# Leaving x un-normalised on chip and applying 1/rms where the products are read, in a hybrid decoder layer

## The chip, the core and the metric

The kernel runs on one core of a Trainium2 chip. The core has five engines, each working through its own queue in order: TensorE (PE in the profile) multiplies matrices, VectorE (DVE) and ScalarE (ACT) work on tiles, GpSimd (POOL) does a few small things, and SyncE (SP) issues most DMAs. An engine goes on only when what its next instruction needs has been signalled. The metric is the device time of one launch in microseconds, median of the runs.

## What is computed

A decoder layer over 256 tokens of width 2048, all in float32. The part that matters here is its entry:

```
h = rms_norm(x, norm_g)                  # x * rsqrt(mean(x*x) + eps) * g, per token
proj = h @ w_in                          # 2048 x 11264
q, k, v, z_a, u_b, v_b, z_b, g_a, g_b = split(proj)
q = rms_norm(q per head, q_norm_g);  k = rms_norm(k per head, k_norm_g)
att = moba_attention(q, k, v)
y_a = (att * silu(z_a)) @ w_proj_a
sgu = spatial_gating(gelu(u_b), gelu(v_b), ...)
y_b = (sgu * silu(z_b)) @ w_proj_b
merged = sigmoid(g_a) * y_a + sigmoid(g_b) * y_b
out = x + merged @ w_out
```

With 256 tokens the attention is plain causal attention inside one block. The factor 1/rms in the first line is one number per token, a row factor, so it can be applied to `x` before the product or to the rows of `proj` after it.

## The kernel before

**Products.** A float32 product is made of three matmuls of halves: every operand is split into a high half (ScalarE's cast to float32r, `wh`, `xh`) and a low half (VectorE's subtraction, `wl`, `xl`), and `three` (L302) issues low by high, high by high, high by low. Weights come as 120 steps of 1 MB (`schedule`, L50). In 104 of them a step is a 2 by 2 set of blocks: for half of these the block products are made as they stand (`direct`, L311: 24 matmuls of 128x512), the other half use seven products instead of eight (`seven`, L325: 21 matmuls), for which VectorE first adds weight blocks (`t`, L143 to L146) and splits more pieces (`wlp`, L155; `tl`, L157).

**Order of steps.** The first eight steps (0 to 7) make q, all direct. Then come k, v, za, vb, ub and zb with eight steps each, g with four chunks that alternate with the projections y, and out. Steps 8 to 15 are k, 16 to 23 are v. While step i is multiplied, step i + 2 is split and step i + 3 is fetched (L664 to L670). Rings of buffers bound how far this runs ahead: four `raw`, three `wh` and `wl`, two `whp` and `wlp`. For ScalarE and VectorE the order up to step 7 is written out by hand (`manual_schedule`, L639); behind it, and for the other engines, a scheduler sets the order when the kernel is built.

**x.** `x` arrives transposed (`xt`, features by tokens). `split_x` (L205) multiplies it by norm_g and splits it into `xuh`, `xul`, which serve q alone. For everything behind q the kernel normalises: `load_nat` (L191) fetches `x` once more by tokens, `stats` (L245) squares and sums it on ScalarE and takes 1/rms (`rsqrt`, L240: VectorE's mean plus eps, then GpSimd's power of -0.5) into `rstd`; `stats_row` (L250) turns `rstd` into a row with two PE transposes (`ps_R`); `normalise` (L258) multiplies `xt` by it in place on VectorE; and `halves_x` (L262) splits the result again into `xh`, `xl`. `forms` and `forms_4` (L272 to L299) make sums of blocks of the normalised `xt` for the seven-product steps. q itself, made from un-normalised halves, gets `rstd` as ScalarE's scale when it is read out (L695).

**Head norms.** `sums` (L376) squares q, k and vb per head on ScalarE and takes rsqrt of the sums; `norm_qk` (L389) applies it.

The dictionary `later`, filled by `at` (L576), says after which step each of these is issued; on SP, the fetch by tokens stands where `load_nat` is called.

Of the kernel before, what the change touches and what calls it, by code (L numbers as in the profile page):

```python
# [13 lines left out]
F32R = mybir.dt.float32r  # L14
# [6 lines left out]
P = 128  # L21
# [46 lines left out]
def hybrid_layer_kernel(  # L68
# [97 lines left out]
    xv = const.tile([P, NVEC + S], F32, name="xv")  # L166
    vec = xv[:, 0:NVEC]
    xt = [slot(F32, f"xt{i}").rearrange("p (k t) -> p k t", t=S) for i in range(2)]
    xu_h, xu_l = [], []

    def load_x(p0, p1):
        nc.sync.dma_start(xt[p0 // 8][:, p0 % 8:(p1 - 1) % 8 + 1, :],
# [20 lines left out]
            nc.sync.dma_start(xn[m], x[m * P:(m + 1) * P, :])  # L193

    for i in range(2):
        xu_h.append(slot(F32R, f"xuh{i}").rearrange("p (k t) -> p k t", t=S))
        xu_l.append(slot(F32R, f"xul{i}").rearrange("p (k t) -> p k t", t=S))

    warm = unit.tile([P, B], BF16, tag="u", name="warm")
    nc.vector.memset(warm, 0.0)  # L200
# [4 lines left out]
    def split_x(kp, js=None):  # L205
        i, a = kp // 4, 2 * (kp % 4)
        for j in js or range(2):
            src = xv[:, NVEC:] if kp + j == 0 else xt[i][:, a + j, :]
            nc.scalar.activation(xt[i][:, a + j, :], src, AF.Copy, scale=vec[:, 2 * kp + j:2 * kp + j + 1])
        sl = slice(a + js[0], a + js[0] + 1) if js else slice(a, a + 2)  # L210
        src = xt[i][:, sl, :]
        nc.scalar.copy(xu_h[i][:, sl, :], src)
        nc.vector.tensor_tensor(xu_l[i][:, sl, :], src, f(xu_h[i][:, sl, :]), op=ALU.subtract)

    ident = const.tile([P, P], F32, name="ident")
    make_identity(nc, ident)
# [17 lines left out]
        nc.sync.dma_start(gain, bass.AP(tensor=sg.tensor, offset=sg.offset, ap=[[0, P], [1, P]]))  # L234

    rstd = const.tile([P, 2], F32, name="rstd")
    R = xv[:, NVEC:]
    ssum = const.tile([P, 2], F32, name="ssum")

    def rsqrt(dst, src, n, count):  # L240
# [4 lines left out]
    def stats():  # L245
        for m in range(2):
            nc.scalar.activation(xn[m], xn[m], AF.Square, accum_out=ssum[:, m:m + 1])
        rsqrt(rstd, ssum, 2, D)

    def stats_row():  # L250
        ps = bank(0, "ps_R")
        for m in range(2):
            nc.tensor.transpose(ps[:, m * P:(m + 1) * P], rstd[:, m:m + 1].to_broadcast([P, P]), ident)
        nc.scalar.copy(R, ps[:, 0:S])

    xh, xl = [None, None], [None, None]

    def normalise(i):  # L258
        src = xt[i]
        nc.vector.tensor_tensor(src, src, R[:, None, :].to_broadcast([P, 8, S]), op=ALU.mult)  # L260

    def halves_x(i):  # L262
        xh[i] = slot(F32R, f"xh{i}").rearrange("p (k t) -> p k t", t=S)
        xl[i] = slot(F32R, f"xl{i}").rearrange("p (k t) -> p k t", t=S)
        nc.scalar.copy(xh[i], xt[i])
        nc.vector.tensor_tensor(xl[i], xt[i], f(xh[i]), op=ALU.subtract)

    def spare(t):

# [104 lines left out]
    def sums(C, name):  # L374
        for m in range(2):
            for c in range(2):  # L376
                ss = small.tile([P, 4], F32, tag="ss", bufs=8, name="ss")
                junk = u("junk")
                for h in range(4):
                    nc.scalar.activation(junk[:, h * P:(h + 1) * P], C[m][c][:, h * P:(h + 1) * P], AF.Square,  # L380
                                         accum_out=ss[:, h:h + 1])
                rs = small.tile([P, 4], F32, tag="rs", bufs=8, name="rs")
                rsqrt(rs, ss, 4, P)
                X["rs", name, m, c] = rs

    def norm_qk(name):
# [17 lines left out]
    def func(name, fn):  # L404
        for m in range(2):
            for c in range(2):
                nc.scalar.activation(X[name][m][c], X[name][m][c], fn)

    def transpose4(b, src, name):
        ps = bank(b, name)  # L410
# [47 lines left out]
    def turn_p(hg, banks):  # L458
        pt = X["PT", hg] = slot(F32, f"PT{hg}")[:, 0:12 * P].rearrange("p (n h t) -> p n h t", n=3, t=P)
        for n, (c, b) in enumerate(((0, 0), (1, 0), (1, 1))):  # L460
            s = X["S0", hg] if c == 0 else X["S1"][:, 4 * hg:4 * hg + 4, :]
            ps = bank(banks[n], f"ps_p{hg}{n}")
            for h in range(4):
                nc.tensor.transpose(ps[:, h * P:(h + 1) * P], s[:, h, b * P:(b + 1) * P], ident)
            nc.scalar.copy(pt[:, n], ps.rearrange("p (h t) -> p h t", t=P))

    def attend(hg, banks):
        v, pt = X["v"], X["PT", hg]
# [114 lines left out]
        fn(*a, free["banks"][n0:n1])  # L583

    i0 = first["q", 0]
    at(i0 + 1, load_nat)
    at(i0 + 2, stats)
    at(i0 + 3, stats_row)
    at(i0 + 3, normalise, 1)
    at(i0 + 4, halves_x, 1)  # L590
    at(i0 + 5, normalise, 0)
    at(i0 + 4, forms_4)
    at(i0 + 5, lambda: forms(xt[0], "x"))
    at(i0 + 6, halves_x, 0)
    at(i0 + 6, halves_f, "x")
    at(i0 + 20, halves_4)
    i0 = first["k", 0]
# [50 lines left out]
        if kp < 2:  # L648
            split(kp, 4)
    def fac(name):  # L650
        if name == "q":
            return xu_h, xu_l
        if name == "out":
            return [X.get(("mh", i)) for i in range(2)], [X.get(("ml", i)) for i in range(2)]
        return xh, xl
# [7 lines left out]
    for i, (kind, name, c, kp, n) in enumerate(G):  # L663
# [8 lines left out]
        if kind == "quad":  # L672
            if n == 0:
                if i and G[i - 1][0] == "quad":

                    E, L = L, E
                Lt = [bank(b, f"acc_{name}{c}_{j}") for j, b in enumerate(L[:3])]
                Et = None
            if len(Lt) == 3 and (plain or not strassen(i)):
                Lt.append(bank(L[3], f"acc_{name}{c}_3"))  # L680
            if strassen(i) and Et is None:
                Et = [bank(b, f"seven_{name}{c}_{j}") for j, b in enumerate(E)]
            if strassen(i):
                last = 4 if name == "g" else SK[-1]
                f8 = "m" if name == "out" else "x"
                seven(Et, Lt, i, kp, kp == SK[0], kp == last, n > 0, *fac(name), X["Fh", f8], X["Fl", f8])
                if kp == last:
                    e = early(Et, f"{name}{c}", xres.get(c) if name == "out" else None)
            else:
                direct(Lt, *fac(name), i, kp, (n == 0, not direct22(i)), n == 7)  # L690
            if n == 7:
                if plain:
                    X[name] = [[u(f"{name}{m}{j}") for j in range(2)] for m in range(2)]
                    for j in range(4):
                        nc.scalar.activation(X[name][j // 2][j % 2], Lt[j], AF.Copy, scale=rstd[:, j // 2:j // 2 + 1])  # L695
                elif name == "out":
                    post_out(c, Lt, e)
                elif name == "g":
                    X["g", c] = final(Lt, e)
                    for m in range(2):  # L700
                        for j in range(2):
                            nc.scalar.activation(X["g", c][m][j], X["g", c][m][j], AF.Sigmoid)
                else:
                    X[name] = final(Lt, e)
        elif kind == "proj":
            if n % 2 == 0:
                Y = (Y if n else []) + [bank(E[n + m], f"y{n}_{c}{m}") for m in range(2)]
            z = ("za", "zb")[n // 2]

            def hl(k, m):  # L710
                return (X[z + "h"][:, k, m * P:(m + 1) * P], X[z + "l"][:, k, m * P:(m + 1) * P])

            mm_rows(Y[n // 2 * 2:], hl, i, None, 4 * (n % 2), n % 2 == 0, n % 2 == 1)
            if n == 3:
                merge(c, Y)
# [68 lines left out]
```

## Time and profile before

| what | value |
|---|---|
| three timed runs | 668.11, 668.73, 669.14 us (median 668.73) |
| span of the profiled execution | 666.6 us |
| PE busy | 653.9 us, 98% of the span, 2982 matmuls |
| DVE busy | 613.9 us, 92% |
| ACT busy | 427.1 us, 64% |
| POOL busy | 30.6 us, 5% |
| HBM read, written | 132.72 MB, 2.10 MB |

The profiled execution's own device time is not given beside its page; its span runs from the first to the last instruction that the profiler saw and is 2.1 us below the median of the timed runs. The profile lists for each engine when an instruction began, how long it took, and, in brackets, how long the engine had sat idle before it and what ended that. Where a line begins with a number such as 29.02, that is the start in microseconds from the span's beginning, and the second number is the duration.

### The profile page before, as it was taken

Reading aid. Unit: us, or ns where it says so; the run is one execution under the profiler, and the core shown is the slowest. Engines: PE = TensorE matmul, PEld = TensorE weight load, DVE = VectorE, ACT = ScalarE, POOL = GpSimd, SP = SyncE. Lnnn points to the kernel's source line nnn. Section 1 sums busy time; section 2 is a strip of 40 time slices with the busy share of each in tenths; the row PEclk is TensorE's granted clock in tenths of the full one; section 3 lists DMA queues with packets and bytes.
Section 4 is the critical chain, followed back from the end, with each engine's and each line's share of the span. In section 5 each row is a group of like instructions: output and inputs, shape, how many; then the busy total and the mean of one; then the engine's idle time right before and its main releaser. Section 6 shows DMA issues by size and latency. Waiting matters only on the chain.

```text
span 666.6 us, 7860 instructions
## 1 busy us (share of the span) xinstructions
PE 653.9 (98%) x2982; PEld 539.5 (81%) x2982; DVE 613.9 (92%) x606; ACT 427.1 (64%) x563; POOL 30.6 (5%) x28
## 2 busy tenths in 40 slices
PE   8799999999999999999999999999999999999997
PEld 4678888888888888888888788888888888888886
DVE  4589999999999699999999999979989989998996
ACT  7778968856895579774656835555564556746460
POOL 1000501300001004000000000000000000000000
PEclk9989999999999999999999999999999999999999
DMA  8962574555455624744546544935583574747641
GB/s 312 418 228 89 220 255 173 198 196 190 166 182 190 252 69 184 276 165 183 197 145 277 210 132 184 329 116 189 190 331 115 191 270 162 252 148 290 200 183 63
DMA packets 22213, 135.32 MB, mean 203 GB/s; under 512 B 2464, under 2 KB 3104, under 8 KB 7072
## 3 DMA queue, kind: packets, MB, share of 16 engines
q1 hardware_dynamic: 21024, 132.73, 54.1%
q10 hardware_dynamic: 1152, 2.10, 1.0%
q8 instruction: 23, 0.38, 0.2%
q14 instruction: 14, 0.11, 0.0%
HBM read 132.72 MB, written 2.10 MB: 202 GB/s over the span
## 4 chain that ended last, share of the span: by engine, by line
PE 75%; DVE 13%; DMA 5%; issue 4%; ACT 2%; SPq 0%; POOL 0%; DVEq 0%; ACTq 0%
PE acc_g L307 12%; PE y L307 11%; PE acc_out L307 9%; PE seven_g L307 6%; PE acc_v L307 4%; PE acc_k L307 4%; PE acc_za L307 4%; PE acc_ub L307 4%; PE acc_q L307 4%; PE seven_out L307 3%; DMA raw<-in_w 3%; DVE tl L157 3%; PE acc_vb L307 3%; DVE wl L126 2%; DMA xnat<-in_x 2%
## 5 line engine op out<-in xcount | busy, mean ns | idle before, releaser
L154 ACT CAST th<-t 128x1024 fp32r<-128x1024 f32 x104 | 109.3, 1054 | 114.1 <-DVE t L143 57.3
L126 DVE TENSOR_TENSOR wl<-raw,wh 128x2048 fp32r<-128x2048 f32 (+2 forms) x76 | 156.1, 2061 | 21.9 <-ACT wh L125 21.7
L125 ACT CAST wh<-raw 128x2048 fp32r<-128x2048 f32 (+2 forms) x76 | 130.8, 1729 | 47.9 <-PE acc_g L307 18.4
L157 DVE TENSOR_TENSOR tl<-t,th 128x1024 fp32r<-128x1024 f32 x104 | 126.2, 1217 | 3.3 <-ACT th L154 3.3
L155 DVE TENSOR_TENSOR wlp<-raw,whp 128x1536 fp32r<-128x1536 f32 x52 | 91.0, 1750 | 7.1 <-ACT whp L152 7.1
L152 ACT CAST whp<-raw 128x1536 fp32r<-128x1536 f32 x52 | 76.8, 1480 | 29.8 <-DMA raw<-in_w 15.1
L143 DVE TENSOR_TENSOR t<-raw 128x1024 f32<-128x1024 f32 x52 | 63.2, 1216 | 0.2
L307 PE MATMUL acc_g<-wl,xh 128*128 128x512 f32 x96 | 37.4, 389 | 0.0
L307 PE MATMUL acc_g<-wh,xh 128*128 128x512 f32 x96 | 37.4, 389 | 0.0
L307 PE MATMUL acc_g<-wh,xl 128*128 128x512 f32 x96 | 37.3, 389 | 0.0
L146 DVE TENSOR_TENSOR t<-t,raw 128x512 f32<-128x512 f32 x52 | 35.8, 689 | 0.3
L145 DVE TENSOR_TENSOR t<-t,raw 128x512 f32<-128x512 f32 x52 | 35.8, 689 | 0.2
L243 POOL TENSOR_TENSOR rs<-ms,mhalf 128x4 f32<-128x4 f32 x12 | 22.4, 1884 | 122.0 <-DVE ms L242 122.0
L307 PE MATMUL acc_q<-wh,xuh 128*128 128x512 f32 x64 | 25.9, 405 | 0.9 <-ACT wh L125 0.9
L307 PE MATMUL acc_q<-wl,xuh 128*128 128x512 f32 x64 | 26.0, 407 | 0.4 <-DVE wl L126 0.4
L307 PE MATMUL y<-wh,zbl 128*128 128x512 f32 x64 | 25.2, 394 | 0.8 <-DVE zbl L507 0.8
L307 PE MATMUL acc_q<-wh,xul 128*128 128x512 f32 x64 | 25.7, 401 | 0.0
L307 PE MATMUL y<-wh,zal 128*128 128x512 f32 x64 | 25.1, 392 | 0.0
L307 PE MATMUL y<-wl,zah 128*128 128x512 f32 x64 | 25.0, 391 | 0.0
L307 PE MATMUL y<-wl,zbh 128*128 128x512 f32 x64 | 24.9, 390 | 0.0
L307 PE MATMUL y<-wh,zbh 128*128 128x512 f32 x64 | 24.9, 390 | 0.0
L307 PE MATMUL acc_out<-wh,mh 128*128 128x512 f32 x64 | 24.9, 389 | 0.0
(502 smaller groups left out, 1598.4 us busy)
## 6 DMA issues: line engine op xcount, KB each, us to landing
raw<-in_w SPq DMA_DIRECT2D x116, 1024.0 KB, 4.8
raw<-in_w SPq DMA_DIRECT2D x7, 512.0 KB, 8.7
xnat<-in_x SPq DMA_DIRECT2D x2, 1024.0 KB, 13.5
xres<-in_x ACTq DMA_DIRECT2D x8, 256.0 KB, 4.7
out<-out_c SPq DMA_DIRECT2D x5, 256.0 KB, 2.5
xt<-in_xT SPq DMA_DIRECT2D x2, 512.0 KB, 8.5
xt<-in_xT SPq DMA_DIRECT2D x3, 256.0 KB, 9.0
raw<-in_w SPq DMA_DIRECT2D x2, 256.0 KB, 4.2
```

What stands on the lines that cost most here:

```text
L125: nc.scalar.copy(h, r)
L126: nc.vector.tensor_tensor(l, r, f(h), op=ALU.subtract)
L143: nc.vector.tensor_tensor(two, r[:, B:3 * B].rearrange("p (a n) -> p a n", a=2), r[:, None, 0:B].to_broadcast([P, 2, B]), op=ALU.add)
L145: nc.vector.tensor_tensor(t[:, 2 * B:3 * B], t[:, 0:B], r[:, 2 * B:3 * B], op=ALU.add)
L146: nc.vector.tensor_tensor(t[:, 3 * B:], t[:, 2 * B:3 * B], r[:, 3 * B:], op=ALU.add)
L152: nc.scalar.copy(wh[i], r[:, B:])
L154: nc.scalar.copy(th[i][:, sl], t[:, sl])
L155: nc.vector.tensor_tensor(wl[i], r[:, B:], f(wh[i]), op=ALU.subtract)
L157: nc.vector.tensor_tensor(tl[i][:, sl], t[:, sl], f(th[i][:, sl]), op=ALU.subtract)
L243: nc.gpsimd.tensor_tensor(dst, ms[:, :n], mhalf[:, :n], op=ALU.pow)
L307: nc.tensor.matmul(acc, a, b, start=(start and n == 0), stop=(stop and n == 2))
```

## The change

1. `normalise`, `halves_x`, `stats_row` and the row `R` are gone. The halves of x times norm_g (`xuh`, `xul`, now called `xh`, `xl` in the code) serve all input products, and `forms`, `forms_4` read the un-normalised `xt`.
2. `rstd` is given as ScalarE's scale where the products are read: in the SiLU and GELU of za, vb, ub, zb (`func`), in the sigmoid of g, in the copies of the transposed attention weights (`turn_p`, which carries v's factor, as v is used un-normalised), and in the squares of k.
3. k's factor from its head norm is multiplied by `rstd` in a new VectorE instruction on 128x4 elements, four times.
4. `load_nat` moves from step 1 to step 3, `stats` from step 2 to step 5.

```diff
-    R = xv[:, NVEC:]
...
-    def stats_row():
-        ps = bank(0, "ps_R")
-        for m in range(2):
-            nc.tensor.transpose(ps[:, m * P:(m + 1) * P], rstd[:, m:m + 1].to_broadcast([P, P]), ident)
-        nc.scalar.copy(R, ps[:, 0:S])
-
-    xh, xl = [None, None], [None, None]
-
-    def normalise(i):
-        src = xt[i]
-        nc.vector.tensor_tensor(src, src, R[:, None, :].to_broadcast([P, 8, S]), op=ALU.mult)
-
-    def halves_x(i):
-        xh[i] = slot(F32R, f"xh{i}").rearrange("p (k t) -> p k t", t=S)
-        xl[i] = slot(F32R, f"xl{i}").rearrange("p (k t) -> p k t", t=S)
-        nc.scalar.copy(xh[i], xt[i])
-        nc.vector.tensor_tensor(xl[i], xt[i], f(xh[i]), op=ALU.subtract)
...
+                scale = rstd[:, m:m + 1] if name == "k" else 1.0
                 for h in range(4):
                     nc.scalar.activation(junk[:, h * P:(h + 1) * P], C[m][c][:, h * P:(h + 1) * P], AF.Square,
-                                         accum_out=ss[:, h:h + 1])
+                                         scale=scale, accum_out=ss[:, h:h + 1])
                 rs = small.tile([P, 4], F32, tag="rs", bufs=8, name="rs")
                 rsqrt(rs, ss, 4, P)
+                if name == "k":
+                    nc.vector.tensor_scalar(rs, rs, scale, None, op0=ALU.mult)
...
-                nc.scalar.activation(X[name][m][c], X[name][m][c], fn)
+                nc.scalar.activation(X[name][m][c], X[name][m][c], fn, scale=rstd[:, m:m + 1])
...
-            nc.scalar.copy(pt[:, n], ps.rearrange("p (h t) -> p h t", t=P))
+            nc.scalar.activation(pt[:, n], ps.rearrange("p (h t) -> p h t", t=P), AF.Copy, scale=rstd[:, b:b + 1])
...
-    at(i0 + 1, load_nat)
-    at(i0 + 2, stats)
-    at(i0 + 3, stats_row)
-    at(i0 + 3, normalise, 1)
-    at(i0 + 4, halves_x, 1)
-    at(i0 + 5, normalise, 0)
+    at(i0 + 3, load_nat)
     at(i0 + 4, forms_4)
     at(i0 + 5, lambda: forms(xt[0], "x"))
-    at(i0 + 6, halves_x, 0)
+    at(i0 + 5, stats)
     at(i0 + 6, halves_f, "x")
...
-                            nc.scalar.activation(X["g", c][m][j], X["g", c][m][j], AF.Sigmoid)
+                            nc.scalar.activation(X["g", c][m][j], X["g", c][m][j], AF.Sigmoid, scale=rstd[:, m:m + 1])
```

How this stands in the queues is seen at three places; numbers at the end of a name belong to the step or are running numbers of the build.

ScalarE in q's stage, before, from the split of x for step 6 on (`wh5` is the high half of step 5's weights, `xnat` x by tokens):

```order
L212 CAST xuh1_100<-xt1_75 128x512
L247 ACTIVATE xnat0_96,ssum_127<-xnat0_96 128x2048
L247 ACTIVATE xnat1_97,ssum_127<-xnat1_97 128x2048
L125 CAST wh5_285<-raw5_244 128x2048
L209 ACTIVATE xt1_75<-xt1_75,xv_73 128x256 x2
L212 CAST xuh1_100<-xt1_75 128x512
L254 COPY xv_73<-ps_R_317 128x256
L125 CAST wh6_324<-raw6_283 128x2048
L265 CAST xh1_352<-xt1_75 128x2048
L125 CAST wh7_363<-raw7_322 128x2048
L125 CAST wh8_399<-raw8_361 128x2048
```

The same place on ScalarE after the change:

```order
L212 CAST xuh1_100<-xt1_75 128x512
L125 CAST wh5_278<-raw5_242 128x2048
L209 ACTIVATE xt1_75<-xt1_75,xv_73 128x256 x2
L212 CAST xuh1_100<-xt1_75 128x512
L125 CAST wh6_314<-raw6_276 128x2048
L259 CAST xuh0_98<-F4_342 128x4x128
L125 CAST wh7_349<-raw7_312 128x2048
L246 ACTIVATE xnat0_96,ssum_127<-xnat0_96 128x2048
L246 ACTIVATE xnat1_97,ssum_127<-xnat1_97 128x2048
L125 CAST wh8_389<-raw8_347 128x2048
L279 CAST Fhx_417<-Fx_377 128x2048
```

The two squarings moved behind the high halves of steps 5, 6 and 7; the copy of the row and the splits of the normalised x are gone.

PE between step 3 and step 4 of q, before (the row that is left out after the change is the second; nothing takes its place):

```order
L307 MATMUL acc_q0_3_181<-wl3_209,xuh0_98 128x512
L253 MATMUL ps_R_317<-ident_113,rstd_126 128x128 x2
L307 MATMUL acc_q0_0_178<-wh4_246,xul1_101 128x512
L307 MATMUL acc_q0_0_178<-wh4_246,xuh1_100 128x512
L307 MATMUL acc_q0_0_178<-wl4_247,xuh1_100 128x512
```

With the transposes of `rstd` gone, no matmul of q's stage reads anything that comes from `stats`.

VectorE where k's head norms are taken, during v's steps, after the change (`ms` is the mean plus eps, `rs` is what GpSimd's power makes of it, `tl19` and `wl20` are low halves of the weights of steps 19 and 20):

```order
L157 TENSOR_TENSOR tl19_883<-t19_876,th19_882 128x1024
L146 TENSOR_TENSOR t19_876<-t19_876,raw19_805 128x512
L241 TENSOR_SCALAR ms_921<-ss_914 128x4
L241 TENSOR_SCALAR ms_932<-ss_925 128x4
L241 TENSOR_SCALAR ms_943<-ss_936 128x4
L241 TENSOR_SCALAR ms_954<-ss_947 128x4
L367 TENSOR_SCALAR rs_920<-rs_920,rstd_126 128x4
L367 TENSOR_SCALAR rs_931<-rs_931,rstd_126 128x4
L367 TENSOR_SCALAR rs_942<-rs_942,rstd_126 128x4
L367 TENSOR_SCALAR rs_953<-rs_953,rstd_126 128x4
L126 TENSOR_TENSOR wl20_961<-raw20_874,wh20_960 128x2048
L157 TENSOR_TENSOR tl19_883<-t19_876,th19_882 128x1024
```

The four products (L367) are new there: each waits for GpSimd's power, and behind them stand `wl20` and the second half of `tl19`, which before stood in the other order.

More of the change, by code (lines that the diff above doesn't have):

```diff
@@ L168, in hybrid_layer_kernel @@
     xt = [slot(F32, f"xt{i}").rearrange("p (k t) -> p k t", t=S) for i in range(2)]
-    xu_h, xu_l = [], []
+    xh, xl = [], []
     def load_x(p0, p1):
@@ L195, in hybrid_layer_kernel @@
     for i in range(2):
-        xu_h.append(slot(F32R, f"xuh{i}").rearrange("p (k t) -> p k t", t=S))
-        xu_l.append(slot(F32R, f"xul{i}").rearrange("p (k t) -> p k t", t=S))
+        xh.append(slot(F32R, f"xuh{i}").rearrange("p (k t) -> p k t", t=S))
+        xl.append(slot(F32R, f"xul{i}").rearrange("p (k t) -> p k t", t=S))
     warm = unit.tile([P, B], BF16, tag="u", name="warm")
@@ L211, in split_x @@
         src = xt[i][:, sl, :]
-        nc.scalar.copy(xu_h[i][:, sl, :], src)
-        nc.vector.tensor_tensor(xu_l[i][:, sl, :], src, f(xu_h[i][:, sl, :]), op=ALU.subtract)
+        nc.scalar.copy(xh[i][:, sl, :], src)
+        nc.vector.tensor_tensor(xl[i][:, sl, :], src, f(xh[i][:, sl, :]), op=ALU.subtract)
     ident = const.tile([P, P], F32, name="ident")
@@ L650, in fac @@
     def fac(name):
-        if name == "q":
-            return xu_h, xu_l
         if name == "out":
```

## The prediction

> **What bounds the kernel now.** I read the page first: engines, then the slices.
>
> ```profile
> PE 653.9 (98%) x2982; PEld 539.5 (81%) x2982; DVE 613.9 (92%) x606; ACT 427.1 (64%) x563; POOL 30.6 (5%) x28
> PE   8799999999999999999999999999999999999997
> PEclk9989999999999999999999999999999999999999
> ```
>
> PE is busy nearly throughout, at full granted clock, but for one dip in the third slice. So nothing is gained except where PE waits or has less to do. PE's own waits, then the chain that ended last from 17 to 58 us, name the dip:
>
> ```profile
> PE ps_R L253 <- POOL rstd L243: 4.9, 1, 4.9
> ```
>
> ```profile
> 17.37 14.11 DMA xnat<-in_x
> ...
> 33.79 0.72 POOL rstd L243
> 34.55 0.43 PE ps_R L253 x2
> 34.98 23.41 PE acc_q L307 x96
> ```
>
> This is the only long wait of PE. The chain runs from the fetch of x by tokens through ScalarE's squares and GpSimd's power to the two transposes of `rstd`, and from there it is PE alone up to 58.4 us. PE's timeline around it gives the price:
>
> ```profile
> 29.23 0.39 PE L307 MATMUL acc_q<-wl,xuh 128*128 128x512 f32 x1
> 34.55 0.43 PE L253 MATMUL ps_R<-ident,rstd 128*128 128x128 f32 x2 [4.93 <-POOL rstd L243]
> 34.74 0.63 PE L307 MATMUL acc_q<-wh,xul 128*128 128x512 f32 x1
> ...
> 38.15 0.48 PE L307 MATMUL acc_q<-wl,xuh 128*128 128x512 f32 x1
> 38.47 0.40 PE L307 MATMUL acc_q<-wh,xul 128*128 128x512 f32 x1
> ...
> 43.04 0.39 PE L307 MATMUL acc_q<-wl,xuh 128*128 128x512 f32 x1
> 43.27 0.39 PE L307 MATMUL acc_q<-wh,xul 128*128 128x512 f32 x1
> ```
>
> Durations overlap, so the starts count. Normally one matmul follows another after 0.227 us (43.04 to 43.27 rounded; 96 matmuls would take 21.8). From 29.23 to 38.47 PE makes ten steps (one of them past the 0.2 us of transposes), which at 0.227 would take 2.27 us; they take 9.24. Besides the standstill, the matmuls from 34.74 to 38.15 stand 0.43 us apart (eight steps in 3.41), half the normal pace, because the clock was lowered after the pause. The dip costs 9.24 - 2.27 = 6.97 us.
>
> **Part by part.**
>
> *The transposes and their wait.* With `ps_R` gone PE goes from step 3 to step 4 with nothing between, if step 4's halves are there; the wait, the transposes and the slow matmuls all go: **-6.97**. What is late next? VectorE and ScalarE in that stage:
>
> ```profile
> 25.10 2.29 DVE L126 TENSOR_TENSOR wl<-raw,wh 128x2048 fp32r<-128x2048 f32 x1 [1.69 <-ACT wh L125]
> 29.02 1.91 ACT L247 ACTIVATE xnat<-xnat 128x2048 f32<-128x2048 f32 x1 [2.49 <-DMA xnat<-in_x]
> 31.50 1.91 ACT L247 ACTIVATE xnat<-xnat 128x2048 f32<-128x2048 f32 x1 [0.48 <-DMA xnat<-in_x]
> 33.41 1.88 ACT L125 CAST wh<-raw 128x2048 fp32r<-128x2048 f32 x1
> ```
>
> Step 4's low half is ready at 27.4, so PE starts it at 29.46, and steps of 24 matmuls (5.44 us) follow at 34.9, 40.3, 45.8 for steps 5 to 7, 51.2 for step 8 and 56.7 for step 9. Step 5's high half stood behind the squares, which waited for x by tokens; now it comes first. Its weights were issued before x by tokens and so are there by 29.0 at the latest if transfers land in order: high half to 30.9, low half (2.3 us) to 33.2, needed at 34.9. Step 6's high half must wait until PE frees a buffer at 29.46 and is done well before 40.3.
>
> *The fetch by tokens and the squares.* On SP the fetch moves behind the weights of step 6:
>
> ```profile
> 16.09 1.61 SPq L193 DMA_DIRECT2D xnat<-in_x  x2
> 19.33 53.67 SPq L111 DMA_DIRECT2D raw<-in_w  x9
> ```
>
> Step 6's weights waited for a free buffer until 19.33, so x is issued at about 20 and 21 instead of 16.1 and 17.4. It landed at 29.0 and 31.5; with 1 MB in front of it (the 2.5 us between those two) I expect 31.5 and 34. Step 7's weights stand behind it and land near 36.5; step 7's high half then ends at 38.4, its low half at 40.7, needed at 45.8. The squares follow on ScalarE, 38.4 to 42.3 (two times 1.9); behind them wait step 8's high half (44.2) and low half (46.5, needed at 51.2), and the halves of the sums of blocks. That is 4.7 us of room: cost 0. The readout of q needs `rstd` only at 51.2.
>
> *Normalising and its halves.* Two VectorE products and two low halves go, and the casts on ScalarE:
>
> ```profile
> 38.32 2.29 DVE L260 TENSOR_TENSOR xt<-xt,xv 128x2048 f32<-128x2048 f32 x1
> 42.73 2.28 DVE L266 TENSOR_TENSOR xl<-xt,xh 128x2048 fp32r<-128x2048 f32 x1
> 40.65 1.92 ACT L265 CAST xh<-xt 128x2048 fp32r<-128x2048 f32 x1 [1.82 <-DVE xt L260]
> ```
>
> That is 2 x 2.29 + 2 x 2.28 = 9.1 us of VectorE, and 2 x 1.92 of ScalarE. PE waited for none of it, so it is worth nothing by itself, but PE comes to k's steps 7 us earlier, and this is what lets VectorE be there too: 9.1 is more than 6.97, and VectorE no longer sits out the squares. Cost 0.
>
> *k's factor: a new wait on VectorE.* The four products by `rstd` wait for GpSimd, and `wl20` and the second half of `tl19` stand behind. Before, the powers were nobody's wait on VectorE:
>
> ```profile
> 99.19 5.44 PE acc_v L307 x24
> ...
> 117.96 2.72 PE seven_v L307 x12
> 114.12 0.37 DVE L242 TENSOR_SCALAR ms<-ss 128x4 f32<-128x4 f32 x4
> 114.83 1.23 DVE L157 TENSOR_TENSOR tl<-t,th 128x1024 fp32r<-128x1024 f32 x1 [0.34 <-ACT th L154]
> 115.97 2.28 DVE L126 TENSOR_TENSOR wl<-raw,wh 128x2048 fp32r<-128x2048 f32 x1
> 33.79 0.71 POOL L243 TENSOR_TENSOR rstd<-ms,mhalf 128x2 f32<-128x2 f32 x1 [30.69 <-DVE ms L242]
> 69.05 8.37 POOL L243 TENSOR_TENSOR rs<-ms,mhalf 128x4 f32<-128x4 f32 x4 [34.55 <-DVE ms L242]
> 114.36 5.90 POOL L243 TENSOR_TENSOR rs<-ms,mhalf 128x4 f32<-128x4 f32 x4 [36.94 <-DVE ms L242]
> ```
>
> Four powers took 5.9 us for k and 8.4 for q, beside a busy VectorE; the one for `rstd`, on half as many columns, took 0.71 while VectorE stood still. After the change VectorE stands still during k's four, so I price the wait by the row that shares this: 4 x 0.71 = 2.8 us; bounds 2.8 and 8.4. [...]
>
> What does PE notice? The 12 matmuls from 117.96 belong to step 19, and the last three, from 120.0, need the second half of `tl19`, which was done at 116.05: 3.95 us of room. Now that half comes later by the wait and by `wl20` in front of it (2.2): 2.8 + 2.2 - 3.95 = 1.05 us too late. Against it stands VectorE's lead. It reached k's `ms` 14.9 us after PE's first v matmul (114.12 - 99.19); with less work it must now wait for PE's last k result, and has from there about 10.5 us of instructions (two steps' `t`, `wlp`, `tl` but for one half). So it gains between 0 and 4.4 us; I take 3. Then PE waits for nothing: cost 0, bounds 0 (2.8 with the lead) and 8.4 + 2.2 - 3.95 = 6.7 (without it). The products themselves are too small to count.
>
> *ScalarE's scales.* 16 squares, 16 SiLU and GELU, 16 sigmoids and 6 copies get a scale from a tile. The same shape with and without one:
>
> ```profile
> 121.00 0.39 ACT L392 ACTIVATE k_h<-k_h,rs 128x128 f32<-128x128 f32 x1
> 100.69 0.30 ACT L380 ACTIVATE junk<-k_c 128x128 f32<-128x128 f32 x1
> 372.00 1.23 ACT L702 ACTIVATE g_c<-g_c 128x512 f32<-128x512 f32 x2 [1.87 <-DVE g_c L365]
> 380.17 0.50 PE L307 MATMUL y<-wh,zbl 128*128 128x512 f32 x1 [0.83 <-DVE zbl L507]
> ```
>
> 0.09 us each, 54 x 0.09 = 4.9 us on an engine busy for 64% that loses 3.84 us of casts. It matters in one place: four sigmoids begin at 372.00, ScalarE's halves of zb come behind them, and PE waits 0.83 us for those at 380.17. There I add 4 x 0.09 = **0.4**; bounds -0.8 (the wait goes) and 1.
>
> *Sum.* Span 666.6 - 6.97 + 0.4 = 660.0. The median of the timed runs is 2.1 above this span; I carry that over: 668.73 - 6.57 = **662.2 us**.
>
> **Rivals.**
>
> *A: the new wait takes part of it back.* The powers stay long (5.9) and VectorE has gained little: PE waits 5.9 + 2.2 - 3.95 = 4.2 us without lead, 1.2 with 3 us. For it: VectorE is busy 92% of the span, and k's steps had no room. Against it: the short power, and the 9.1 us. The time lies between 663.4 and 666.4; middle 665.
>
> *B: slower.* k's powers take as long as q's (8.4) and VectorE has no lead: `tl19` is 6.7 us late. A pause longer than the present one (4.93) would be followed by matmuls at half pace, as at 34.74: nine steps, 9 x 0.2 = 1.8 us. That is 8.5 against 6.97: 662.2 + 8.5 = 670.7. It decides against the change from a PE pause of about 5 us on (5.0 + 1.8 + 0.4 is over 6.97). Against it: both conditions must hold.
>
> *C: the squares come late.* If x by tokens landed 5 us later than 34, step 8's halves, queued behind the squares, would make PE wait at 51.2. For it: transfers are issued closely there. Against it: 4.7 us of room. Some 3 us of loss: 665.
>
> *D: ScalarE becomes the limit.* All 4.9 us of new scales come onto the path: 668.73 - 6.97 + 4.9 = 666.7. Against it: 64% busy, and 3.84 us of casts gone.
>
> *E: nothing happens*, because the scheduler brings another wait into q's stage at once: 668.7. Against it: the order on PE shows nothing between steps 3 and 4.
>
> **How the numbers follow.** Forecast 0.68 (662.2, its own range 660.8 to 663.4), A 0.17, B 0.05, C 0.04, D 0.03, E 0.03. Low end: -6.97 and the 0.8 us wait at 380 gone, 668.73 - 7.8 = 660.9, set to 660.8. The high end takes in A without lead but not D: 666.0, which leaves out D, B, E and a part of A, about 0.15, beside little at the low end. Differences within 0.2% (1.3 us) cannot be told from none. Faster: forecast, A, C and D but for a part, 0.91; same: E and the edge of A and B, 0.04; slower: B, 0.05.
>
> **What would show it.** Right: no wait of PE between 29 and 52 us, PE reaching k's first matmul near 51.2 instead of 58.4, granted clock full in the third slice, GpSimd's four k powers in about 3 us with VectorE idle beside them, no PE wait at step 19, the squares near 38. A: PE idle some microseconds before the `seven_v` matmuls near 113, released by `tl`. C: PE idle near 51, released by `wl`. The forecast would be wrong if PE's lead of 7 us over the present trace, there at k's first matmul, were smaller at the last one by more than a microsecond.

## The result and the profile after

The changed kernel takes 665.28 us (median of four runs, 664.48 to 666.85) where the kernel before takes 668.59 beside it; the ratio is 0.9949, with a 95% interval of 0.9933 to 0.9965. That is 3.3 us faster; the forecast was 6.5 (662.2). The profiled execution is the one of 664.48 us, with a span of 662.8; the kernel before had 666.6.

The page of the changed kernel, engines and slices:

```profile
PE 652.3 (98%) x2980; PEld 538.4 (81%) x2980; DVE 606.6 (92%) x606; ACT 427.3 (64%) x560; POOL 27.2 (4%) x28
...
PE   8999999999999999999999899999999999999997
...
PEclk9999999999999999999999999999999999999999
```

The dip in the third slice is gone, and there is a small new one in the 23rd (364 to 381 us). PE's waits, in total, times and the longest:

```profile
PE acc_g L288 <- ACT wh L125: 1.8, 1, 1.8
...
PE ps_s L419 <- DVE S L426: 1.1, 1, 1.1
PE seven_vb L288 <- DVE za_c L464: 0.5, 1, 0.5
```

The wait on `rstd` has left the list, and so has y's wait for zb (0.8). The first two of these are new, the third stood at 0.2 before. Where they cost is seen when PE's first matmul of each step is compared between the two traces:

| PE begins | before | after | lead |
|---|---|---|---|
| step 5 (q) | 41.91 | 34.98 | 6.93 |
| step 19 (v) | 116.43 | 109.50 | 6.93 |
| step 20 (v) | 121.19 | 114.57 | 6.62 |
| step 26 (za, behind the attention scores) | 159.51 | 154.27 | 5.24 |
| step 36 (vb) | 218.47 | 213.89 | 4.58 |
| step 65 (y, first chunk) | 372.31 | 367.72 | 4.59 |
| step 67 | 385.78 | 381.87 | 3.91 |
| last matmul | 662.21 | 658.35 | 3.86 |

So the whole 6.93 us are won in q's stage, and 3.1 are given back: 0.31 at step 19, 1.4 at the scores, 0.3 at the copies of the attention weights, 0.3 in step 34, 0.7 at y. The first two lie behind k's new product. VectorE's timeline there:

```profile
105.72 0.38 DVE L241 TENSOR_SCALAR ms<-ss 128x4 f32<-128x4 f32 x4
107.00 0.23 DVE L367 TENSOR_SCALAR rs<-rs,rstd 128x4 f32<-128x4 f32 x1 [0.91 <-POOL rs L242]
107.98 0.23 DVE L367 TENSOR_SCALAR rs<-rs,rstd 128x4 f32<-128x4 f32 x1 [0.75 <-POOL rs L242]
108.95 0.23 DVE L367 TENSOR_SCALAR rs<-rs,rstd 128x4 f32<-128x4 f32 x1 [0.74 <-POOL rs L242]
109.93 1.83 DVE L367 TENSOR_SCALAR rs<-rs,rstd 128x4 f32<-128x4 f32 x1 [0.75 <-POOL rs L242]
110.07 2.29 DVE L126 TENSOR_TENSOR wl<-raw,wh 128x2048 fp32r<-128x2048 f32 x1
```

And GpSimd's powers for 1/rms, q and k:

```profile
43.51 0.71 POOL L242 TENSOR_TENSOR rstd<-ms,mhalf 128x2 f32<-128x2 f32 x1 [40.41 <-DVE ms L241]
60.06 6.50 POOL L242 TENSOR_TENSOR rs<-ms,mhalf 128x4 f32<-128x4 f32 x4 [15.84 <-DVE ms L241]
105.96 3.93 POOL L242 TENSOR_TENSOR rs<-ms,mhalf 128x4 f32<-128x4 f32 x4 [39.40 <-DVE ms L241]
```

k's powers are regular, one product about every 0.98 us, with VectorE standing (beside a VectorE at work the same four took 5.90 us in the kernel before); from the beginning of `ms` to that of `wl` 4.35 us pass, and for 3.15 of them VectorE is idle. (The four rows of `rs` are the products; the last one's 1.83 us overlap `wl`.)

How a stop at 106 reaches the scores at 152 is seen only beside a trace without the stop, that of `pe_order_again` below. There `wl` begins at 106.49, 3.58 us earlier. First the changed kernel, the two fetches of weights on SP's queue that follow, and what ScalarE and VectorE do with the second:

```profile
113.52 0.33 SPq L111 DMA_DIRECT2D raw<-in_w  x1
122.72 0.33 SPq L111 DMA_DIRECT2D raw<-in_w  x1
127.43 1.91 ACT L125 CAST wh<-raw 128x2048 fp32r<-128x2048 f32 x1 [1.30 <-DMA raw<-in_w]
129.37 2.29 DVE L126 TENSOR_TENSOR wl<-raw,wh 128x2048 fp32r<-128x2048 f32 x1 [1.00 <-ACT wh L125]
151.70 0.72 DVE L426 COPY_PREDICATED S<-tri,ps_s 128x512 f32<-128x512 uint8 x1
```

The same five instructions in `pe_order_again`:

```profile
109.94 0.33 SPq L111 DMA_DIRECT2D raw<-in_w  x1
119.15 0.33 SPq L111 DMA_DIRECT2D raw<-in_w  x1
124.30 1.91 ACT L125 CAST wh<-raw 128x2048 fp32r<-128x2048 f32 x1 [1.75 <-PE acc_v L289]
126.25 2.29 DVE L126 TENSOR_TENSOR wl<-raw,wh 128x2048 fp32r<-128x2048 f32 x1 [1.37 <-ACT wh L125]
148.87 0.73 DVE L424 COPY_PREDICATED S<-tri,ps_s 128x512 f32<-128x512 uint8 x1
```

A fetch waits for one of the four `raw` buffers (the sums `t` lie in the same ring), and VectorE frees it with `tl`. So its stop of 3.6 us puts both fetches 3.6 us later. The cast at 127.43, which otherwise waits for PE, then waits for the transfer, and VectorE reaches the masked copies of the scores 2.8 us later. VectorE has slack there in both traces (1.0 and 1.37 us of waiting for the cast); the lateness goes through the ring of buffers, past that slack.

The loss at y, in PE's timeline:

```profile
374.09 0.39 PE L288 MATMUL y<-wl,zah 128*128 128x512 f32 x1
376.29 0.50 PE L288 MATMUL acc_g<-wh,xul 128*128 128x512 f32 x1 [1.81 <-ACT wh L125]
376.62 0.39 PE L288 MATMUL y<-wh,zbl 128*128 128x512 f32 x1
```

ScalarE's row for that cast:

```profile
374.33 1.90 ACT L125 CAST wh<-raw 128x2048 fp32r<-128x2048 f32 x1 [0.41 <-PE y L288]
```

The scheduler has put one matmul of step 68 (`acc_g`) ahead of the second half of y. Its weights' cast waits for a buffer that PE itself frees at 374.3, so PE cannot come to it before the cast's 1.9 us have passed, however early everything else is: from 374.09 to 376.29 its starts lie 2.2 us apart, and for 1.81 of them it is idle.

### The profile page after: what moved, and what is told of

It reads as the page before. It is cut to its first block, busy times and chain, and to the rows that moved or that the text cites. A ratio compares the mean times of both kernels' runs of the same rounds, so it can differ in the third digit from the quotient of the medians.

```text
span 662.8 us, 7853 instructions
## 1 busy us (share of the span) xinstructions
PE 652.3 (98%) x2980; PEld 538.4 (81%) x2980; DVE 606.6 (92%) x606; ACT 427.3 (64%) x560; POOL 27.2 (4%) x28
## 4 chain that ended last, share of the span: by engine, by line
PE 83%; DVE 8%; ACT 3%; DMA 2%; issue 2%; SPq 0%; DVEq 0%; ACTq 0%
PE acc_g L288 16%; PE y L288 13%; PE acc_out L288 9%; PE seven_g L288 8%; PE acc_q L288 6%; PE acc_ub L288 5%; PE acc_zb L288 5%; PE acc_k L288 5%; PE seven_out L288 3%; PE acc_vb L288 3%; DMA raw<-in_w 2%; PE acc_v L288 2%; DVE tl L157 2%; PE seven_zb L288 2%; PE seven_ub L288 2%
## 5 line engine op out<-in xcount | busy, mean ns | idle before, releaser
L288 PE MATMUL acc_g<-wh,xul 128*128 128x512 f32 x96 | 37.5, 390 | 1.8 <-ACT wh L125 1.8
L288 PE MATMUL acc_g<-wl,xuh 128*128 128x512 f32 x96 | 37.3, 389 | 0.0
L288 PE MATMUL acc_g<-wh,xuh 128*128 128x512 f32 x96 | 37.3, 389 | 0.0
L288 PE MATMUL y<-wh,zah 128*128 128x512 f32 x64 | 25.0, 391 | 0.0
L288 PE MATMUL acc_out<-wl,mh 128*128 128x512 f32 x64 | 24.9, 389 | 0.0
```

The costliest lines, as they stand in the source:

```text
L288: nc.tensor.matmul(acc, a, b, start=(start and n == 0), stop=(stop and n == 2))
```

## The experiments

In what follows "lead" is PE's lead over the kernel before, as in the table. The kernels were timed in five groups, each with the kernel before beside it; its medians were 669.51, 668.86, 668.55, 668.38 and 668.87 us. A ratio is to the kernel before of the same group. Where the lead stands at the beginning of step 5 differs by how q's first matmuls start, from 5.8 to 7.3 us in the profiles of kernels with the change; what counts is how it goes on from there.

### Which part makes the gain

`before_late` is the kernel before with only its stage moved later, as the change moves the fetch and the squares; it still normalises:

```diff
-    at(i0 + 1, load_nat)
-    at(i0 + 2, stats)
-    at(i0 + 3, stats_row)
-    at(i0 + 3, normalise, 1)
-    at(i0 + 4, halves_x, 1)
+    at(i0 + 3, load_nat)
+    at(i0 + 4, stats)
+    at(i0 + 5, stats_row)
+    at(i0 + 5, normalise, 1)
+    at(i0 + 5, halves_x, 1)
```

(`forms_4` goes from step 4 to 5 with them.)

> The kernel before with its normalising kept, but with the fetch by tokens, the squares, the row, the normalising and the halves moved two steps later, as far as the changed kernel's fetch and squares: PE then meets the transposes behind step 5. Theory (moving alone does not do, VectorE's 9.1 us of normalising and halves must go too): no wait at the transposes, but step 8's halves stand on VectorE behind the normalising and its halves and end near 59 instead of 51, so PE waits about 8 us there: 667 to 670. Rival (the early wait was the whole cost, the order suffices): 662 to 664.

Measured: 670.36 us, ratio 1.0014 (1.0005 to 1.0024). Its wait:

```profile
PE acc_k L307 <- DVE wl L126: 5.3, 1, 5.3
```

The lead is 6.45 us at step 8 and gone at step 9: the work that was moved out of q's stage makes VectorE late for k, and behind the wait the first two matmuls last 0.79 and 0.63 us, where those ahead of it last 0.39. Moved alone, at these steps, the stage gains nothing.

`stats_early` is the reverse, the change with the fetch and the squares put back:

```diff
-    at(i0 + 3, load_nat)
+    at(i0 + 1, load_nat)
+    at(i0 + 2, stats)
...
-    at(i0 + 5, stats)
```

> The changed kernel with the fetch of x by tokens put back at step 1 and the squares at step 2, in front of the high half of step 5, the factors staying. Theory (what empties TensorE's queue at 29 to 38 us is VectorE's normalising and halving, not the place of the fetch alone; but the fetch in front delays step 5's high half, and the squares stand in front of ScalarE's casts): a wait of 1 to 2.7 us comes back at step 5 and the time is 666.3 to 668 (ratio 0.996 to 0.9985). Rival (the late fetch is worth nothing by itself): no wait there, ratio as the changed kernel's. Other rival (the late fetch is all of the gain): 668.6 or more, ratio 1.

Measured: 668.01 us, ratio 0.9995 (0.9983 to 1.0008), 2.8 above the changed kernel in the same group (665.18, ratio 0.9946) and slower than expected. PE's waits:

```profile
PE acc_q L288 <- DVE wl L126: 1.8, 2, 1.6
...
PE acc_v L288 <- DVE k_h L337: 0.9, 1, 0.9
```

In its profile the lead falls to 4.55 in step 5, as expected, and to 3.33 in v's first step. So neither half does it alone: the late fetch without less work gains nothing, and less work without the late fetch gains too little to be told from nothing. By its time alone `stats_early` would suit the rival that the late fetch is all of the gain; `before_late` excludes that.

### k's factor

`k_pow2` takes each of k's powers twice (`times` is 2 for k alone), which only lengthens the new wait.

```diff
-        nc.gpsimd.tensor_tensor(dst, ms[:, :n], mhalf[:, :n], op=ALU.pow)
+        for _ in range(times):
+            nc.gpsimd.tensor_tensor(dst, ms[:, :n], mhalf[:, :n], op=ALU.pow)
```

> Each of k's four powers is computed twice in a row, so that VectorE's wait for GpSimd grows from about 4 to about 8 us; the order is unchanged and so is the output. Theory (VectorE's wait sets the path): the 4 us come onto the path in full, PE waits about 4.3 us at step 19 and nothing more at the scores, 669.3, no better than the kernel before. Rival (the loss at step 19 and at the scores has another cause): there is room, 665.3 to 666.

Measured: 671.53 us, ratio 1.0024 (1.0013 to 1.0036). PE stands 4.1 us where it lost 0.3, at the place that the prediction named:

```profile
117.85 0.79 PE L289 MATMUL seven_v<-tl,Fhx 128*128 128x512 f32 x1 [4.05 <-DVE tl L157]
118.44 0.63 PE L289 MATMUL acc_v<-th,xul 128*128 128x512 f32 x1
```

and the matmuls behind go at half pace, 0.43 us apart, for 5.6 us (granted clock 0.50 from 117.9 to 123.5). Four powers more cost 5.2 us by the two ratios (1.0024 against the change's 0.9946 in the next group), and the time is 2.2 us above the expected one, which had left out the half pace. The wait is real and its room was used up.

`k_eps` takes the wait away. Since the mean of (k/rms)^2 is mean(k^2)/rms^2, the factor moves into the epsilon, eps times (mean(x^2) + eps), one number per token; the product and the squares' scale go (one more VectorE instruction on 128x2 makes the new epsilon in `stats`):

```diff
-                rsqrt(rs, ss, 4, P)
-                if name == "k":
-                    nc.vector.tensor_scalar(rs, rs, scale, None, op0=ALU.mult)
+                rsqrt(rs, ss, 4, P, ssum[:, m:m + 1] if name == "k" else EPS)
```

> The factor 1/rms of k is folded into its head norm's epsilon (mean of squares of un-normalised k, plus epsilon times the token's mean square of x), so the four products on VectorE and their wait for GpSimd's powers are gone, and the squares of k carry no scale; the output is the same. Theory (the wait on VectorE, about 4 us from 106.1 to 110.1, makes VectorE late up to the attention scores): PE keeps its lead of 6.9 us through v's steps and the scores, the losses of 0.3 us in step 19 and 1.35 us at the scores go, and the later ones (0.3 at the attention weights, 0.3 at za, 0.7 at the zb transposes) stay: about 1.65 us faster than the changed kernel, 663.6. Rival (VectorE has too much work in v's steps anyway): the loss at the scores stays, 665.0. Rival (ScalarE's scales): only the 16 squares get shorter, 665.0 to 665.3.

`k_pool` keeps the product, but on GpSimd, behind its powers:

```diff
-                    nc.vector.tensor_scalar(rs, rs, scale, None, op0=ALU.mult)
+                    nc.gpsimd.tensor_tensor(rs, rs, scale.to_broadcast([P, 4]), op=ALU.mult)
```

> The four products of k's factor by 1/rms are made on GpSimd behind its powers instead of on VectorE; the squares keep their scale, the order of every engine is otherwise that of the changed kernel. Theory (VectorE's wait): as without the product, 1.65 us faster than the changed kernel, 663.6, though ScalarE's norms of k come some us later. Rival (ScalarE's scales, the scheduler's order): no difference, 665.3.

Measured: 665.32 us (0.9945, 0.9933 to 0.9958) and 666.16 (0.9949, 0.9937 to 0.9962): neither is faster than the change itself. In `k_eps`'s profile nothing is lost at step 19 or at the scores (lead 6.16 from step 5 to 34), but 2.4 us are lost at y. The gap there is the same 2.2 us, and this time the matmuls behind it are slow. The granted clock (the column behind the engines) in that stretch of `k_eps`:

```profile
376.40:379.60 3.20, 3.20 (x10) 2.49 (x9) 3.20 (x3) 1.64 (x2) 0.00 (x0) 0.53 0.23 54
```

and in the changed kernel, the same time behind its gap:

```profile
377.30:380.50 3.20, 3.20 (x15) 2.63 (x14) 3.20 (x3) 1.70 (x2) 0.00 (x0) 1.00 0.27 46
```

In `k_pool` VectorE no longer waits for the powers, but ScalarE does:

```profile
ACT k_c L376 <- POOL rs L367: 2.7, 2, 1.5
```

and VectorE then waits 1.7 us for a cast of ScalarE's. Step 19 loses nothing, the scores lose 1.5 us as in the change, and y loses 2.9, at half clock as in `k_eps` (0.50 from 377.5 to 380.0). Both expectations (663.6) missed by 1.7 and 2.6 us, because of y and, in `k_pool`, of the scores.

### The order at y

Four kernels, in two groups (`after_again` and `pe_order` in one, the other two in the next). `after_again` is the changed kernel as it is. `pe_order` is `k_eps`, and `after_order` the changed kernel, with PE's order of steps 66 to 68 as written; the one matmul goes back behind y. `pe_order_again` repeats `pe_order` beside `after_order`.

```diff
+        if i == 66:
+            kept = ExitStack()
+            kept.enter_context(tc.manual_schedule(engines={mybir.EngineType.PE}))
+        if i == 69:
+            kept.close()
```

> The changed kernel as it is, beside the three kernels of this call on the same chip, so that they are compared with it and not only with the kernel before. Both theories: ratio to the kernel before 0.993 to 0.9965, as measured. It shows also whether the second 2.19 us gap of TensorE at y0 is in every profile, and whether the matmuls behind it run at half pace (0.43 us apart) in this one, which they did not in the changed kernel's first profile (its fastest run).

> As the one with k's factor in epsilon, but with TensorE's order of steps 66 to 68 as written, so that the one matmul of step 68 (acc_g of wh68) stands behind y2's and not in front of them. Theory (the order costs: that matmul waits for a cast that itself waits for TensorE): the wait on acc_g of wh68 is gone, TensorE stands about 1.3 us at y0 rather than 2.2, the matmuls behind keep full pace, and the end comes 0.6 to 2 us earlier: 663.4 to 664.8 where the kernel before has 668.6 to 669.5 (ratio 0.992 to 0.9935). Rival (the gap is y's own: the sigmoids and zb are late whatever stands in front): the wait goes over to zb, the gap stays at 2 us or more, and the time is that of the one with k's factor in epsilon, ratio 0.9945.

> The changed kernel with TensorE's order of steps 66 to 68 as written and nothing else; k's factor stays on VectorE. Theory (two separate losses, 1.7 us at step 19 and the scores behind k's powers, 1.5 to 3 us at y0 behind the one matmul that came forward): y0's part comes back, k's part stays: 663 to 664 where the kernel before has 668.6 to 669.5 and the one with both mended 661.9 (ratio 0.9915 to 0.993). Rival (what is saved ahead of y0 is lost at y0 whatever the order, so that k's part costs nothing by then): as the one with both mended, 661.9, ratio 0.990. Other rival (the order alone does nothing): 665.2, ratio 0.9945.

> The kernel with k's factor in epsilon and TensorE's order of steps 66 to 68 as written, once more, for a direct comparison with the one that has the order alone, and for a profile that is not its slowest execution. Theory: ratio 0.990 again; in the profile TensorE's lead over the kernel before is near 6.9 us from step 5 through step 65 and at the end.

| kernel | median, us | ratio (95%) |
|---|---|---|
| `after_again` | 665.18 | 0.9946 (0.9934 to 0.9959) |
| `pe_order` | 661.91 | 0.9902 (0.9884 to 0.9920) |
| `after_order` | 664.10 | 0.9934 (0.9921 to 0.9946) |
| `pe_order_again` | 662.16 | 0.9914 (0.9894 to 0.9934) |

In the profile of `pe_order_again` PE's wait at y is the old one, for the half of zb, and short:

```profile
372.91 0.50 PE L289 MATMUL y<-wh,zbl 128*128 128x512 f32 x1 [0.76 <-DVE zbl L489]
```

Its lead is 7.11 us from step 5 to the scores, 6.73 from step 36, and 7.20 at the end. `after_order` keeps the loss at step 19 and the scores (lead 6.51, then 4.21) and loses nothing at y (3.61 before it, 3.86 behind). So the two losses are separate: the order costs 0.8 us by the ratios and 1.1 by the medians (of two groups, and the intervals overlap; in the profiles the lead falls by 0.7 at y in the change and rises by 0.3 in `after_order`), k's factor 1.3 and 1.9 (in one group). But k's part shows only where y is mended. Without that, `k_eps` in its profile spends at y, at half clock (0.53), what it has saved. `pe_order` beats both kernels of this case, by 3.3 us over the change in the same group, and by more than expected (663.4 to 664.8). In 3 of its 11 timed executions, though, it takes 664.7 to 664.9, in the others 661.1 to 662.5.

### ScalarE's scales

`noscale` is `pe_order` without the scales; 1/rms is missing for v, za, ub, vb, zb and g.

```diff
-                nc.scalar.activation(X[name][m][c], X[name][m][c], fn, scale=rstd[:, m:m + 1])
+                nc.scalar.activation(X[name][m][c], X[name][m][c], fn)
```

(and in the same way in the sigmoid of g and the copies of the attention weights)

> As the one with TensorE's order of steps 66 to 68 as written, and ScalarE's scale of 1/rms left out at v, za, ub, vb, zb's sigmoids, g and the copies of the attention weights, so that those results lack the factor. It prices ScalarE's scales. Theory (they are off TensorE's path but for the few where ScalarE is late: the weights' copies at steps 31 to 33, za, y0's four sigmoids): 0.4 to 1 us below that kernel. Rival (54 scales at 0.09 us each lie on the path): 4 to 5 us below it.

Measured: 660.92 us, ratio 0.9895 (0.9875 to 0.9915), 1.0 below `pe_order`; the fastest executions differ by the same (660.51 and 661.53), the ratios by 0.5, with intervals that overlap. In its profile the 0.4 us that `pe_order_again` loses in step 34 are not there; but `pe_order_again` makes that up again at y, so that from step 5 to the end its lead grows by 0.1 us and that of `noscale` by 0.4. So the scales cost between 0.3 and 1.0 us, not 4 to 5.

### The executions 3 us later

The profile of `pe_order` itself is one of these (664.85 us). GpSimd's second power there:

```profile
108.64 6.98 POOL L242 TENSOR_TENSOR rs<-ms,mhalf 128x4 f32<-128x4 f32 x1
```

and what VectorE and ScalarE did beside it:

```profile
107.93 2.28 DVE L126 TENSOR_TENSOR wl<-raw,wh 128x2048 fp32r<-128x2048 f32 x1
...
114.07 0.68 DVE L145 TENSOR_TENSOR t<-t,raw 128x512 f32<-128x512 f32 x1
117.91 1.23 DVE L157 TENSOR_TENSOR tl<-t,th 128x1024 fp32r<-128x1024 f32 x1 [3.16 <-ACT th L154]
...
115.65 1.28 ACT L374 ACTIVATE k_c<-k_c,rs 128x128 f32<-128x128 f32 x4 [4.36 <-POOL rs L242]
```

The power was issued while `wl` ran, and ended at 115.62, 0.87 us after VectorE stopped at 114.75. In `pe_order_again` the second power ended at 109.64, 0.86 us after `wl` ended at 108.78:

```profile
107.10 2.54 POOL L242 TENSOR_TENSOR rs<-ms,mhalf 128x4 f32<-128x4 f32 x1
106.49 2.29 DVE L126 TENSOR_TENSOR wl<-raw,wh 128x2048 fp32r<-128x2048 f32 x1
```

So each of these two powers, issued while `wl` ran, ended 0.86 or 0.87 us after the end of a VectorE instruction: in `pe_order_again` the first such end, in `pe_order` the fifth. That they were held off until then is the author's reading of these times. ScalarE waits for the power (4.36 us), and VectorE, in the end, for ScalarE (3.16).

The power is not all of it, though. This execution ends 3.7 us behind that of `pe_order_again`, and 1.3 of them are there long before the power: PE's lead is 5.78 us from step 5 on instead of 7.11. PE stops for q's first halves at 10.25 us (0.87, for a cast that waited for its transfer) and, more briefly, up to 15.4. The same matmul behind that in `pe_order` and in `pe_order_again`:

```profile
15.71 0.40 PE L289 MATMUL acc_q<-wh,xul 128*128 128x512 f32 x1
14.38 0.39 PE L289 MATMUL acc_q<-wh,xul 128*128 128x512 f32 x1
```

Behind the power 2.6 us are lost, in v's steps and at the scores, where `pe_order_again` loses nothing.

`pow_one` puts k's sixteen sums into one tile, for one power in place of four, VectorE not waiting (`pe_order` otherwise):

```diff
+            nc.gpsimd.tensor_tensor(rs, ms, mhalf, op=ALU.pow)
```

> As the one with k's factor in epsilon and TensorE's order of steps 66 to 68 as written, but k's sixteen sums lie in one tile, so that GpSimd takes one power of 128x16 where it took four of 128x4. By the rows so far 128x2 takes 0.71 and 128x4 1.01 us, 0.15 for each element of a partition: the one power takes about 2.9 us where VectorE stands, against 4.0 for the four, and ScalarE cannot begin with the first factors before its end. In that kernel's profiles the four took 5.8 us beside VectorE in the fast execution (661.1) and 9.9 in the slow one (664.9), where one of them alone took 7.0. Theory (the slow executions come from single powers that fall badly beside VectorE's instructions; one power falls badly less often than four, or as often): fewer executions at 664.7 to 664.9, the fast ones at 661 to 662; median 661.0 to 662.2. Rival (the slow executions come from the start-up or a late transfer): as many slow ones as before, 1 in 3, whatever the power takes. Other rival (a power beside VectorE is stretched in proportion to its length): it takes 8 to 10 us each time, and every execution is at 664 or more.

Measured: 662.64 us, ratio 0.9938 (0.9913 to 0.9963): seven executions at 661.1 to 662.7, five at 667.2 to 668.0. Late ones are not fewer, as the theory had it, but as frequent as its first rival said (the start or a late transfer), and they are later, by 5.6 us (667.5 against 662.0) instead of 3.1. Its profile is an early one; the power came before `wl` and took 2.90 us although VectorE worked from then on, and `wl` was not slower for it:

```profile
106.25 2.90 POOL L371 TENSOR_TENSOR rs<-ms,mhalf 128x16 f32<-128x16 f32 x1 [39.60 <-DVE ms L369]
106.91 2.29 DVE L126 TENSOR_TENSOR wl<-raw,wh 128x2048 fp32r<-128x2048 f32 x1 [0.74 <-ACT wh L125]
```

A late one of this kernel was not profiled.

`pow_one_held` has the one power, with the change's product on VectorE behind it, so that VectorE stands (`after_order` otherwise):

```diff
+            nc.vector.tensor_scalar(ms, ss, 1.0 / P, EPS, op0=ALU.mult, op1=ALU.add)
+            nc.gpsimd.tensor_tensor(rs, ms, mhalf, op=ALU.pow)
+            for m in range(2):
+                half = rs[:, 8 * m:8 * m + 8]
+                nc.vector.tensor_scalar(half, half, rstd[:, m:m + 1], None, op0=ALU.mult)
```

> The changed kernel with TensorE's order of steps 66 to 68 as written and k's sixteen sums in one tile: one power of 128x16, and the product by 1/rms on VectorE as in the change, in two instructions, so that VectorE stands until the power is done. Theory: a power that begins while a VectorE instruction runs is held off until VectorE stops or leaves a gap (in the slow profile it ended 0.87 us after VectorE's stop), and that makes the executions 3 to 6 us slower where VectorE does not wait. Here VectorE stands, so the power takes 2.9 us every time, VectorE stands 1.0 us less than with four powers (4.0), none of the executions is more than 1.5 us above the fastest, and the time is 663.0 to 663.6 where the kernel before has 668.5 and the one with four powers and that order 664.1. Rival (the slow executions come from something else): 1 in 3 is 3 to 6 us above the rest here too. Other rival (the length of the stand does not count, any wait there costs the same): 664.1.

Measured: 663.52 us, ratio 0.9915 (0.9902 to 0.9929), executions from 662.63 to 664.01. GpSimd's and VectorE's rows:

```profile
106.20 2.90 POOL L369 TENSOR_TENSOR rs<-ms,mhalf 128x16 f32<-128x16 f32 x1 [39.64 <-DVE ms L368]
...
109.14 0.93 DVE L372 TENSOR_SCALAR rs<-rs,rstd 128x8 f32<-128x8 f32 x2 [3.02 <-POOL rs L369]
```

Against four powers (`after_order`) that is 0.6 us less by the medians and 1.3 by the ratios; the intervals overlap, so it is likely and not shown to be faster. In its profile step 19 loses nothing (the lead stays 7.07 us up to the scores), the scores still lose 1.4. None of the ten executions of these two kernels is 1.5 us above its fastest. If 1 in 3 were late there too, that would come about in 2 of 100 cases. But in the changed kernel itself, where VectorE stands too and y's order is not mended, one execution of four lies 2.4 us above the fastest and one of five 1.7. That a long power (6.98 us) makes an execution late is shown in one profile, for 2.6 of its 3.7 us; that such a power makes the late ones in general is argued from these counts, and late transfers at the start remain as a rival.

## Why the prediction was right or wrong

The sign, the place of the gain and its size there were right; what it costs elsewhere was put too low, so that the time came out 3.1 us above the forecast, outside the forecast's own range (660.8 to 663.4) and inside the whole one, where rival A had its middle (665). The sign by which the forecast would be wrong came too: PE's lead was 3.1 us smaller at the last matmul than at k's first, not within a microsecond. That the whole range held is in part luck: 0.7 us of the loss, at y, belongs to no rival.

- *The dip in q's stage, -6.97.* Right: the lead is 6.93 us from step 5 on (6.73 in `after_again`), PE begins k at 51.30 (51.2 was forecast), and nothing is late next. The fetch by tokens was issued at 19.8 (20 was forecast) and the squares ran at 38.39 (38.4).
- *Normalising and its halves, 0 by itself.* Right, and needed: with them kept the same move gains nothing (`before_late`).
- *k's factor, 0.* Wrong, and this is the step that failed: "4 x 0.71 = 2.8". The row it was taken from has two elements a partition (0.71 us); with four a power took 1.01 us, with sixteen 2.90, so here the price went with the elements, and the four took 3.93. The trace before had a row of the right size, which the line of four together hides; the timeline from 114.2 to 115.3 us shows the first alone:

  ```profile
  114.36 1.01 POOL L243 TENSOR_TENSOR rs<-ms,mhalf 128x4 f32<-128x4 f32 x1 [36.94 <-DVE ms L242]
  ```

  "I take 3" for VectorE's lead was wrong too: `ms` came 13.5 us behind PE's first v matmul (105.72 - 92.26) instead of 14.9, a gain of 1.5. By the prediction's own sum that makes 3.93 + 2.2 - 3.95 - 1.5 = 0.68 us at step 19; 0.31 was measured. What the step left out altogether is larger: it looked at the next consumer only, and not at the ring of buffers that the waiting engine frees. That cost 1.4 us at the scores.
- *Short powers while VectorE stands.* Right: k's four took 3.93 us with VectorE standing, 5.90 beside a VectorE at work in the kernel before. One power issued while `wl` ran took 2.54 us in `pe_order_again` and 6.98 in `pe_order`, against 1.01. Why they are longer there no run shows.
- *ScalarE's scales, +0.4 at y alone.* The size was inside its bounds (0.3 to 1.0 us by `noscale`, bounds -0.8 to 1), the place wrong. At y the wait for zb is 0.76 us in `pe_order_again`, no longer than before; the loss is in step 34 (0.3 to 0.4, gone in `noscale`). The 0.3 at the copies of the attention weights is there only where the scores come late, and not in `pe_order_again`. What y lost in the change has another cause, an order of the scheduler that the prediction had not looked up behind q and k.
- *The median's 2.1 us over the span.* It is 1.7 in the profiled execution, which is also the fastest of the four; the rest of the distance from 4.1 us (this execution) to 3.3 (the medians) lies in executions that were not profiled.

*The rivals.* A had the number and half the mechanism: a new wait took part of the gain back, but through the scores and the scheduler's order, with only 0.3 us before the `seven_v` matmuls near 113. B did not come, but `k_pow2` shows its mechanism: twice the powers, and PE's pause (4.05 us) with matmuls at half pace behind it (0.43 us apart) makes the kernel slower. C, D and E did not come. With both losses taken away (`pe_order`) the gain is 6.4 to 7.0 us, the forecast's.

## What to carry to other kernels

A wait put on an engine that feeds others is not priced at its next consumer alone (here 0.31 us there and 1.4 further on): follow the buffers that the engine frees, to the fetches that wait for them, and from there to the next place without slack. Price a small operation by a row of its own size, and look for rows of it beside a busy engine too: a power of 1.01 us took 2.23 to 6.98 here when issued while VectorE's `wl` ran. Letting that engine wait may be the steadier choice, which the counts here suggest and do not show. When a change lets TensorE run earlier, read the built order at every place where it waited before, since one matmul put forward cost 0.8 to 1.1 us here.

## What the runs showed of the hardware

- A GpSimd power took 0.71, 1.01 and 2.90 us for 2, 4 and 16 elements a partition with VectorE standing (the kernel before at 33.79, the changed kernel at 105.96, `pow_one_held` at 106.20). One of 4 elements issued while VectorE's `wl` (2.29 us) ran took 2.23, 2.79 and 2.89 us in the kernel before, 2.54 in `pe_order_again` and 6.98 in `pe_order`; each ended 0.86 to 0.87 us after the end of a VectorE instruction, in `pe_order` not of the first. Issued while a shorter one ran (`tl`, `t`), it took 1.16 to 2.05 in the kernel before. One of 16 elements issued just before `wl` ran on beside it in its 2.90, and `wl` in its 2.29 (`pow_one`).
- After a PE pause of 2.2 us at y (from start to start, 1.8 of it idle) the granted clock fell to 0.53 from 376.4 to 379.6 in the profile of `k_eps` and to 0.50 from 377.5 to 380.0 in that of `k_pool`; the slow matmuls begin 1.3 and 1.1 us after PE had resumed. In the profiles of the changed kernel (twice) it stayed at 1.00. In `k_pool` the pause lay only 0.1 us later than in the change's first profile (374.20 to 376.39 against 374.09 to 376.29). What decides between the two no run shows. After the longer waits, of 4.93 us in the kernel before and of 4.05 in `k_pow2`, the clock was 0.50 from 34.9 to 37.9 and from 117.9 to 123.5.
